# A two-block transformer on one core: the first MLP matrices with both parts of x side by side, and the crossings between layers cut in two

## The chip, the core and the metric

The kernel runs on one NeuronCore of a Trainium2 chip. The metric is the device time of one execution in microseconds (us); lower is better. TensorE multiplies a stationary 128x128 operand (loaded by its own instruction, the weight load) with a moving operand of up to 512 columns and writes to PSUM, whose banks hold 512 fp32 values per partition. VectorE (DVE), ScalarE (ACT) and GpSimd (POOL) do the rest, and SyncE (SP) starts the transfers of the weights.

## The reference, cut to what matters

Two blocks run one after the other on 256 tokens of width 1024. The first has two layers, each a mixer (a convolution with latent attention, then a sparse attention) followed by an MLP; the second puts 16 meta tokens in front and has two more layers. Everything is float32. What the change touches is the MLP and the step between two layers:

```python
def sq_relu_mlp(x, w1, w2):
    h = jax.nn.relu(x @ w1)
    return (h * h) @ w2
...
        x = x + rms_norm(m, norm_mix_post[layer])
        h = rms_norm(x, norm_mlp_pre[layer])
        x = x + rms_norm(sq_relu_mlp(h, mlp_w1[layer], mlp_w2[layer]), norm_mlp_post[layer])
```

w1 is 1024x4096 and w2 is 4096x1024; there are two such MLPs.

## The kernel before

**Products in parts.** For accuracy each fp32 number a is split into a high part (rounded to the format fp32r that TensorE takes) and a low part (the rest), and a product is the sum of three: high by high, high by low, low by high. `mm3` issues these three. Each weight tile of 128x1024 comes in by DMA, ScalarE rounds it to its high part (L288) and VectorE subtracts to get the low one (L289). `Stream` keeps four such tiles ready.

**The MLP** (`mlp`, from L606). Activations stand transposed: 128 features on the partitions, 256 tokens in the columns, in eight slices `xh[:, k]` and `xl[:, k]`. The hidden layer has 16 pieces j of 256 features. For one piece, two tiles m times eight slices k times three products of 256 columns run into one PSUM bank "d" (`take2`, 48 products). `hidden` then squares what is positive (Relu and Square on ScalarE, a product and a subtraction on VectorE) and leaves the high and low operands `hh`, `hl`. `acc_block` multiplies a piece with its rows of w2: 24 products of 512 columns into four accumulators in the "w" banks. Pieces 0 to 3 are made before the first `acc_block`; from then on piece j+1 is made ahead of `acc_block` j. In the last block the four accumulators finish one after the other (two halves of the tokens, two halves of the features), and `done` has ScalarE square each with a sum (L479).

**The crossing** (`cross`). When a layer's product is complete, each half of the tokens (t = 0, 1: 128 tokens each) is normalised, transposed back on TensorE and added to x, and from the new x come the next layer's `xh`, `xl`. For a half: VectorE adds the sums into `q` (L501 or L503), GpSimd raises it to -1/2 (L504), ScalarE and VectorE scale one 256-column half each of the two accumulators (L506, L508, and DVE calls by the helper at L493), TensorE does eight 128-column transposes into two banks (L514), `busy` puts idle products of 512 columns behind the last real one (2 in the first half, 4 in the second), and VectorE adds eight 128-column pieces to x (helper `after`, L493: it keeps VectorE's calls in the written order). All eight adds of the first half stand ahead of the second half's scaling. Then, slice by slice, ScalarE makes `xh` (L527) and VectorE `xl`.

There are four crossings: 1 from the first layer into the first MLP, 2 from that MLP into the third layer, 3 from the third layer into the second MLP, 4 from that MLP into the second block.

**The order of the work.** Each engine runs its own queue in order. The queues are laid out when the program is built, by a scheduler that goes by the written order and by estimated times, so an instruction that it expects to be ready late is put behind later ones.

**Where xh and xl live.** Two tiles with one buffer each, allocated by `xg("xh", ...)` and `xg("xl", ...)`.

## Time and profile before

| | us |
|---|---|
| median of three runs | 980.37 |
| lowest and highest | 979.43, 981.09 |
| the profiled execution, its own time | 979.38 |
| its span, from the first to the last instruction | 977.6 |

The span lies 1.8 us inside the execution's own time. Busy time of an engine is a union of its instructions' times; TensorE's instructions overlap each other, so the time from one start to the next, not an instruction's length, is what a product costs.

### The profile page before, as it was taken

How to read it: one execution, taken by the hardware profiler on the slowest of the kernel's cores; microseconds unless marked ns; L12 is line 12 of the kernel's file. 1: busy time of each engine (PE TensorE's matmuls, PEld its weight loads, DVE VectorE, ACT ScalarE, POOL GpSimd, SP SyncE). 2: the span in 40 equal slices, each digit the busy share in tenths (PEclk: the TensorE clock that was granted, in tenths of full speed). 3: DMA queues.
4: the chain of work that ended last, by engine and by line, in shares of the span. 5: the costliest groups of instructions: out<-in, count | busy, mean ns of one | idle time of the engine just before them, and what ended most of it. 6: DMA issues, size and time to landing. Idle time of an engine off the chain costs nothing.

```text
span 977.6 us, 17239 instructions
## 1 busy us (share of the span) xinstructions
PE 950.6 (97%) x6674; PEld 852.8 (87%) x6674; DVE 662.5 (68%) x1358; ACT 513.6 (53%) x929; POOL 83.6 (9%) x117
## 2 busy tenths in 40 slices
PE   7999999999999999998999999999999999999996
PEld 6999879999998898876989999978898789998985
DVE  6889567555554999983855555567988757657762
ACT  6646456444444677773744444454535435363442
POOL 1121000000000100000000000000211210005121
PEclk9999999999999999999999999999999999999999
DMA  9754436655554455430666555536354314633201
GB/s 333 250 172 151 134 126 234 223 187 186 193 190 138 144 193 154 141 103 1 203 210 194 188 187 187 191 103 248 110 183 141 120 45 145 221 130 129 89 2 43
DMA packets 46066, 154.52 MB, mean 158 GB/s; under 512 B 6424, under 2 KB 7968, under 8 KB 45856
## 3 DMA queue, kind: packets, MB, share of 16 engines
q1 hardware_dynamic: 45552, 152.85, 47.6%
q8 instruction: 52, 0.85, 0.3%
q10 hardware_dynamic: 432, 0.57, 0.2%
q14 instruction: 30, 0.25, 0.1%
HBM read 152.34 MB, written 2.70 MB: 159 GB/s over the span
## 4 chain that ended last, share of the span: by engine, by line
PE 94%; ACT 2%; DVE 2%; issue 1%; DMA 1%; POOL 0%; SPq 0%; POOLq 0%; ACTq 0%
PE pd L327 47%; PE pw L327 38%; PE pm L327 5%; PE pm L1133 1%; DVE x L493 1%; PE pm L1165 1%; ACT st L288 1%; DMA x<-in_xT 1%; PE pm L1521 0%; PE pw L514 0%; PE pm L1723 0%; PE pm L514 0%; PE pw L875 0%; ACT sq L479 0%; ACT pm L1119 0%
## 5 line engine op out<-in xcount | busy, mean ns | idle before, releaser
L289 DVE TENSOR_TENSOR st<-st,st 128x1024 fp32r<-128x1024 f32 (+2 forms) x274 | 330.0, 1214 | 161.2 <-ACT st L288 160.6
L288 ACT ACTIVATE st<-st 128x1024 fp32r<-128x1024 f32 (+2 forms) x274 | 282.1, 1042 | 271.7 <-PE pd L327 164.2
L327 PE MATMUL pd<-xh,st 128*128 128x256 f32 (+1 forms) x1856 | 360.2, 289 | 9.1 <-ACT st L288 6.1
L327 PEld LDWEIGHTS pd<-xh,st 128*128 128x128 f32 x1856 | 297.3, 192 | 16.8 <-ACT st L288 6.1
L327 PE MATMUL pd<-xl,st 128*128 128x256 f32 (+1 forms) x928 | 267.5, 289 | 0.0
L327 PEld LDWEIGHTS pd<-xl,st 128*128 128x128 f32 x928 | 178.2, 192 | 3.8 <-issue 0.9
L327 PE MATMUL pw<-st,hh 128*128 128x512 f32 x512 | 157.4, 390 | 0.0
L327 PEld LDWEIGHTS pw<-st,hh 128*128 128x128 f32 x512 | 94.3, 188 | 18.1
L327 PE MATMUL pw<-st,hl 128*128 128x512 f32 x256 | 98.9, 389 | 0.0
L327 PE MATMUL pd<-akq,st 128*128 128x272 f32 (+1 forms) x384 | 78.0, 293 | 0.0
L327 PE MATMUL pw<-xh,st 128*128 128x256 f32 (+1 forms) x384 | 73.6, 286 | 0.0
L327 PEld LDWEIGHTS pd<-akq,st 128*128 128x128 f32 x384 | 61.0, 189 | 2.3 <-issue 1.9
L327 PEld LDWEIGHTS pw<-xh,st 128*128 128x128 f32 x384 | 61.0, 190 | 0.5 <-issue 0.3
L327 PEld LDWEIGHTS pw<-st,hl 128*128 128x128 f32 x256 | 48.1, 188 | 10.3
L327 PE MATMUL pd<-gs,st 128*128 128x272 f32 (+1 forms) x192 | 55.3, 288 | 0.0
L327 PE MATMUL pw<-xl,st 128*128 128x256 f32 (+1 forms) x192 | 54.8, 286 | 0.0
L388 POOL TENSOR_TENSOR rc<-rc,mhalf 128x2 f32<-128x2 f32 (+4 forms) x13 | 13.9, 1074 | 307.0 <-DVE rc L385 307.0
L327 PE MATMUL pw<-st,mh 128*128 128x512 f32 x128 | 38.0, 402 | 1.3 <-ACT mh L339 1.3
L327 PEld LDWEIGHTS pw<-xl,st 128*128 128x128 f32 x192 | 36.5, 190 | 0.2 <-DVE xl L493 0.2
L327 PEld LDWEIGHTS pd<-gs,st 128*128 128x128 f32 x192 | 36.2, 189 | 0.5 <-issue 0.4
L1119 ACT ACTIVATE pm<-pm,st 128x128 f32<-128x128 f32 (+1 forms) x64 | 28.4, 446 | 4.4 <-DVE st L1117 4.3
L327 PEld LDWEIGHTS pw<-st,mh 128*128 128x128 f32 x128 | 23.3, 188 | 6.9 <-ACT mh L339 2.2
(465 smaller groups left out, 1282.7 us busy)
## 6 DMA issues: line engine op xcount, KB each, us to landing
st<-in_w SPq DMA_DIRECT2D x128, 512.0 KB, 4.6
st<-in_ab_in SPq DMA_DIRECT2D x32, 512.0 KB, 4.3
st<-in_cd_in SPq DMA_DIRECT2D x28, 512.0 KB, 4.3
st<-in_a_in SPq DMA_DIRECT2D x18, 512.0 KB, 6.5
st<-in_c_in SPq DMA_DIRECT2D x16, 512.0 KB, 4.7
st<-in_a_out SPq DMA_DIRECT2D x8, 512.0 KB, 4.9
st<-in_c_out SPq DMA_DIRECT2D x8, 512.0 KB, 4.5
st<-in_ab_out SPq DMA_DIRECT2D x8, 512.0 KB, 4.3
```

What stands on the lines that cost most here:

```text
L288: self.last = self.nc.scalar.activation(hi[:, p], raw[:, p], AF.Copy).ins
L289: self.nc.vector.tensor_tensor(lo[:, p], raw[:, p], hi[:, p].bitcast(F32), op=OP.subtract)
L327: self.pe = self.nc.tensor.matmul(out, lhsT, rhs, start=start, stop=stop, skip_group_check=True).ins
L388: nc.gpsimd.tensor_tensor(r, r, self.mhalf[:p, :n], op=OP.pow)
L493: prev = f(*args, **kw).ins
L1119: nc.scalar.activation(o, o, AF.Exp, scale=-1.0, bias=st[:, 0, t, b:b + 1], accum_out=st[:, 1, t, b:b + 1])
L1133: nc.tensor.transpose(tp[:, 128 * j:128 * j + 128], src, self.ident)
L1165: nc.tensor.transpose(ps[:b - a, 128 * j:128 * j + 128], x[:, a:b], self.ident)
```

## The change

In both MLPs, pieces 4 to 15 of the hidden layer are made by a new function `wide`. `xh` and `xl` become the two halves of one tile `xx`, so that one product of 512 columns gives high-by-high in the first half of a bank and high-by-low in the second; low-by-high stays a product of 256 columns. Each of the two tiles m has a bank of its own, and its two halves are added on the way out. Relu and square become one VectorE instruction.

In the crossings, the first half's scaling and transposes (`turn(0)`) are issued by `done` as soon as the first two accumulators are squared, in the written order ahead of the last accumulators' products. Both scalings of the first half are whole 512-column instructions on VectorE; in the second half ScalarE does one and VectorE the other. There are three idle products in place of six. Three of the first half's adds stand ahead of the second half, the other five are spread over the slices.

```diff
-BUSY = (2, 4)
+BUSY, EARLY = 3, 3
...
-    def xg(self, tag, dt, n):
-        t = self.xgp.tile([128, 8 * T2], dt, tag=tag, name=tag)
-        return t[:, :8 * n].rearrange("p (k n) -> p k n", k=8)
+    def xg(self, dt, n):
+
+        t = self.xgp.tile([128, 2, 8 * T2], dt, tag="xx", name="xx")
+        self.xx = t[:, :, :8 * n].rearrange("p a (k n) -> p a k n", k=8)
+        return self.xx[:, 0], self.xx[:, 1]
...
         self.ms.append((m, acc))
...
+        if i == 1:
+            self.scratch = self.psum("d")
+            self.half = self.turn(0)
+
+    def turn(self, t):
+
+        nc = self.nc
+        q = self.np_.tile([128, 8], F32, tag="rc", name="rc", bufs=6)[:, :1]
+        a, b = self.sums[:, 2 * t:2 * t + 1], self.sums[:, 2 * t + 1:2 * t + 2]
+        if self.post[2]:
+            nc.vector.scalar_tensor_tensor(q, a, b, self.eps[:, t:t + 1], op0=OP.add, op1=OP.add)
+        else:
+            nc.vector.tensor_scalar(q, a, b, EPS, op0=OP.add, op1=OP.add)
+        nc.gpsimd.tensor_tensor(q, q, self.mhalf[:, :1], op=OP.pow)
+        (m0, a0), (m1, a1) = self.ms[2 * t:2 * t + 2]
+
+        if t:
+            nc.scalar.activation(m0, a0, AF.Copy, scale=q)
+        else:
+            nc.vector.tensor_scalar(m0, a0, q, None, op0=OP.mult)
+        self.scaled = nc.vector.tensor_scalar(m1, a1, q, None, op0=OP.mult).ins
+        ps = [self.psum("mw"[t]) for _ in range(2)]
+        for p, m in zip(ps, (m0, m1)):
+            for k in range(4):
+                nc.tensor.transpose(p[:, 128 * k:128 * k + 128], m[:, 128 * k:128 * k + 128], self.ident)
+        return ps
...
+        self.busy(BUSY)
+        first = self.half
+        for k in range(EARLY):
+            new(0, first, k)
+        second = self.turn(1)
+        prev = self.scaled
         self.sqs, self.tiles = [], (T_SEQ, meta)
-        new(0)
-        new(1)
+        both = lambda k: [new(0, first, k) for _ in range(k >= EARLY)] + [new(1, second, k)]
+        both(0)
+        both(1)
         for k in range(8):
             if k < 6:
-                new(k + 2)
+                both(k + 2)
...
+            def wide(j):
+
+                hi, lo = self.st.take()
+                a = mp.tile([128, 2, SEQ], F32, tag="a", name="a")
+                for m in range(2):
+                    z = self.psum("d").rearrange("p (t n) -> p t n", t=2)
+                    for k in range(8):
+                        s = slice((m * 8 + k) * 128, (m * 8 + k) * 128 + 128)
+                        self.mm(z, hi[:, s], xx[:, :, k], k == 0, False)
+                        self.mm(z[:, 0], lo[:, s], xh[:, k], False, k == 7)
+                    c = mp.tile([128, SEQ], F32, tag="zc", name="zc")
+                    nc.scalar.activation(c, z[:, 1], AF.Copy)
+                    nc.vector.tensor_tensor(a[:, m], z[:, 0], c, op=OP.add)
+                h = mp.tile([128, 2, SEQ], F32, tag="h", name="h")
+                nc.vector.scalar_tensor_tensor(h, a, 0.0, a, op0=OP.max, op1=OP.mult)
+                hh = mp.tile([128, 2, SEQ], F32R, tag="hh", name="hh", bufs=4)
+                hl = mp.tile([128, 2, SEQ], F32R, tag="hl", name="hl", bufs=4)
+                self.hilo(hh, hl, h)
+                hs[j] = (hh, hl)
...
                 if 4 <= j + 1 < 16:
-                    hidden(j + 1, self.take2(1, xh, xl)[0])
+                    wide(j + 1)
...
-            mh, ml = self.xg("xh", F32R, T2), self.xg("xl", F32R, T2)
+            mh, ml = self.xg(F32R, T2)
...
-            xh, xl = self.xg("xh", F32R, SEQ), self.xg("xl", F32R, SEQ)
-            x = self.cross(x, gain((2, 4, 6)[j]), xh, xl, eps=self.eps if j % 2 else None)
+            xh, xl = self.xg(F32R, SEQ)
+            x = self.cross(x, gain((2, 4, 6)[j]), xh, xl)
```

The other uses of `xg`, in the second block's layers, take the two halves of the one tile in the same way.

## Rows read from the trace of the kernel before

**Rows 1.** The profile page, part 1 (busy us, share of the span, instructions of each engine) and the engines' shares of part 4 (the chain of work that ended last).

```profile
PE 950.6 (97%) x6674; PEld 852.8 (87%) x6674; DVE 662.5 (68%) x1358; ACT 513.6 (53%) x929; POOL 83.6 (9%) x117
...
PE 94%; ACT 2%; DVE 2%; issue 1%; DMA 1%; POOL 0%; SPq 0%; POOLq 0%; ACTq 0%
```

**Rows 2.** The chain of work that ended last, in order of time: start us, length us, what ran, and how many instructions. A block of the first MLP's first matrix and one of its second matrix; the two last blocks of the second matrix; a piece in the second block's first layer whose products have 272 columns.

```profile
176.71 5.70 PE pd L327 x48
182.41 5.46 PE pw L327 x24
...
305.17 10.91 PE pw L327 x48
...
714.39 6.21 PE pd L327 x48
```

**Rows 3.** The timeline of crossing 1 (from the first layer into the first MLP): start us, length us, engine, line, operation, output<-input, shapes, count, and in brackets the idle time before it with what ended it.

```profile
127.56 0.55 POOL L504 TENSOR_TENSOR rc<-rc,mhalf 128x1 f32<-128x1 f32 x1 [14.51 <-DVE rc L501]
...
129.07 1.52 PE L327 MATMUL pd<-st 128*128 128x512 f32 x6
129.27 0.60 ACT L479 ACTIVATE sq<-pw 128x512 f32<-128x512 f32 x1
...
129.99 0.21 DVE L501 TENSOR_SCALAR rc<-ss 128x1 f32<-128x1 f32 x1
...
130.28 0.55 POOL L504 TENSOR_TENSOR rc<-rc,mhalf 128x1 f32<-128x1 f32 x1 [2.17 <-DVE rc L501]
130.43 1.03 PE L514 MATMUL pm<-cg,sq 128*128 128x128 f32 x8
130.87 0.48 ACT L506 ACTIVATE sq<-pw,rc 128x256 f32<-128x256 f32 x1 [0.91 <-POOL rc L504]
...
131.29 1.39 DVE L493 SCALAR_TENSOR_TENSOR x<-pm,gains,x 128x128 f32<-128x128 f32 x5 [1.08 <-PE pm L514]
...
133.36 0.87 DVE L493 TENSOR_SCALAR sq<-pw,rc 128x256 f32<-128x256 f32 x2
...
134.37 0.87 DVE L493 SCALAR_TENSOR_TENSOR x<-pw,gains,x 128x128 f32<-128x128 f32 x3
...
135.31 0.65 PE L327 MATMUL pd<-xh,st 128*128 128x256 f32 x2 [0.59 <-ACT xh L527]
```

**Rows 4.** Busy time by stretch, around the first products behind crossings 1, 2, 3 and 4: for each engine busy us and instructions, then the granted TensorE clock (1.00 is 2.4 GHz, 0.50 is 1.2 GHz), the DMA engines' share and GB/s.

```profile
134.00:140.00 6.00, 5.41 (x29) 4.81 (x30) 5.80 (x17) 5.16 (x12) 0.00 (x0) 0.72 0.23 93
320.00:326.00 6.00, 5.39 (x38) 4.39 (x39) 5.80 (x18) 4.69 (x11) 0.00 (x0) 1.00 0.00 0
462.00:468.00 6.00, 5.39 (x31) 5.10 (x31) 5.94 (x18) 5.80 (x13) 0.00 (x0) 0.72 0.00 0
650.00:656.00 6.00, 6.00 (x35) 5.68 (x35) 6.00 (x17) 5.61 (x13) 0.00 (x0) 0.72 0.46 147
```

**Rows 5.** The timeline of TensorE alone, behind crossing 1, while the clock is at 1.2 GHz.

```profile
136.86 0.41 PE L327 MATMUL pd<-xh,st 128*128 128x256 f32 x1
137.07 0.41 PE L327 MATMUL pd<-xl,st 128*128 128x256 f32 x1
```

**Rows 6.** Groups of instructions by line and shape, from 148.6 to 315.9 us (the first MLP): busy us, mean ns of one, idle before.

```profile
L618 DVE TENSOR_TENSOR h<-a 128x512 f32<-128x512 f32 x16 | 10.9, 684 | 0.0
L621 ACT ACTIVATE hh<-a 128x512 fp32r<-128x512 f32 x16 | 10.1, 632 | 0.4
...
L616 ACT ACTIVATE a<-pd 128x512 f32<-128x512 f32 x14 | 8.1, 580 | 0.0
```

**Rows 7.** Busy time by stretch, 50 us of the first MLP; columns as in rows 4.

```profile
200.00:250.00 50.00, 50.00 (x332) 46.05 (x332) 27.23 (x26) 23.33 (x27) 0.00 (x0) 1.00 0.58 190
```

**Rows 8.** The timelines of ScalarE and of VectorE at the last block of the first MLP: the start and the end of what makes its last pair of operands.

```profile
306.05 0.58 ACT L616 ACTIVATE a<-pd 128x512 f32<-128x512 f32 x1
...
308.11 0.69 DVE L622 TENSOR_TENSOR hl<-h,hh 128x512 fp32r<-128x512 f32 x1
```

**Rows 9.** The timeline of crossing 2 (from the first MLP into the third layer).

```profile
315.91 1.52 PE L327 MATMUL pd<-st 128*128 128x512 f32 x6
...
316.27 1.95 POOL L915 MEMSET kl<- 64x1024 f32 x2 [0.42 <-PE pw L327]
...
318.88 0.54 POOL L504 TENSOR_TENSOR rc<-rc,mhalf 128x1 f32<-128x1 f32 x1
...
322.16 0.51 PE L327 MATMUL pd<-xh,st 128*128 128x256 f32 x2 [0.59 <-ACT xh L527]
```

**Rows 10.** The timeline of crossing 3 (from the third layer into the second MLP).

```profile
455.25 1.53 PE L327 MATMUL pd<-st 128*128 128x512 f32 x6
...
456.34 0.54 POOL L504 TENSOR_TENSOR rc<-rc,mhalf 128x1 f32<-128x1 f32 x1 [5.57 <-DVE rc L501]
...
457.20 0.21 DVE L501 TENSOR_SCALAR rc<-ss 128x1 f32<-128x1 f32 x1 [0.94 <-ACT sq L479]
...
462.67 0.50 PE L327 MATMUL pd<-xh,st 128*128 128x256 f32 x2 [0.59 <-ACT xh L527]
```

**Rows 11.** The timeline of crossing 4 (from the second MLP into the second block).

```profile
644.01 1.53 PE L327 MATMUL pd<-st 128*128 128x512 f32 x6
...
645.29 0.54 POOL L504 TENSOR_TENSOR rc<-rc,mhalf 128x1 f32<-128x1 f32 x1 [2.25 <-DVE rc L503]
...
650.26 0.39 PE L327 MATMUL pw<-xh,st 128*128 128x272 f32 x1
```

More of the change, by code (lines that the diff above doesn't have):

```diff
@@ L486, in cross @@
+    def cross(self, x, g2, xh, xl, meta=None):
+        nc = self.nc
+        g, name = self.post[:2]
         if name:
             self.xn = self.xt(SEQ, name)
-        xn, prev = self.xn, None
+        xn, prev = self.xn, self.scaled
         def after(f, *args, **kw):
             nonlocal prev
-            with self.tc.issue_after(prev) if prev is not None else nullcontext():
+            with self.tc.issue_after(prev):
                 prev = f(*args, **kw).ins
-        self.scratch = self.psum("d")
@@ L496, in cross @@
-        for t, banks in enumerate(("mm", "ww")):
-            q = self.np_.tile([128, 8], F32, tag="rc", name="rc", bufs=6)[:, :1]
-            a, b = self.sums[:, 2 * t:2 * t + 1], self.sums[:, 2 * t + 1:2 * t + 2]
-            if eps is None:
-                nc.vector.tensor_scalar(q, a, b, EPS, op0=OP.add, op1=OP.add)
-            else:
-                nc.vector.scalar_tensor_tensor(q, a, b, eps[:, t:t + 1], op0=OP.add, op1=OP.add)
-            nc.gpsimd.tensor_tensor(q, q, self.mhalf[:, :1], op=OP.pow)
-            (m0, a0), (m1, a1) = self.ms[2 * t:2 * t + 2]
-            nc.scalar.activation(m0[:, 0:256], a0[:, 0:256], AF.Copy, scale=q)
-            after(nc.vector.tensor_scalar, m0[:, 256:512], a0[:, 256:512], q, None, op0=OP.mult)
-            nc.scalar.activation(m1[:, 0:256], a1[:, 0:256], AF.Copy, scale=q)
-            after(nc.vector.tensor_scalar, m1[:, 256:512], a1[:, 256:512], q, None, op0=OP.mult)
-            ts = slice(128 * t, 128 * t + 128)
-            ps = [self.psum(c) for c in banks]
-            for h, (p, m) in enumerate(zip(ps, (m0, m1))):
-                for k in range(4):
-                    nc.tensor.transpose(p[:, 128 * k:128 * k + 128], m[:, 128 * k:128 * k + 128], self.ident)
-            self.busy(BUSY[t])
-            new = lambda k: after(nc.vector.scalar_tensor_tensor, xn[:, k, ts], ps[k // 4][:, 128 * (k % 4):128 * (k % 4) + 128],
-                                  g[:, k:k + 1], x[:, k, ts], op0=OP.mult, op1=OP.add)
-            if t == 0:
-                for k in range(8):
-                    new(k)
@@ L521, in cross, with new @@
+        def new(t, ps, k):
+            ts = slice(128 * t, 128 * t + 128)
+            after(nc.vector.scalar_tensor_tensor, xn[:, k, ts], ps[k // 4][:, 128 * (k % 4):128 * (k % 4) + 128],
+                  g[:, k:k + 1], x[:, k, ts], op0=OP.mult, op1=OP.add)
+        self.busy(BUSY)
[4 more added lines that the diff above has]
+        prev = self.scaled
         self.sqs, self.tiles = [], (T_SEQ, meta)
-        new(0)
@@ L1566, in layer_cd @@
             nc.sync.dma_start(ccd, self.i["ccd"])
-            big = self.xg("xl", F32, T2).rearrange("p a b -> p (a b)")
+            place, big = [v.rearrange("p a b -> p (a b)") for v in self.xg(F32, T2)]
             dect, ck = [big[:, a:b].rearrange("p (k n) -> p k n", n=T2) for a, b in ((0, 4 * T2), (4 * T2, 6 * T2))]
@@ L1583, in layer_cd @@
             nc.gpsimd.memset(zero, 0.0)
-            big = self.xg("xh", F32, T2).rearrange("p a b -> p (a b)")
-            dkr = big[:, :4 * T2].rearrange("p (k n) -> p k n", n=T2)
-            dq = big[:, 4 * T2:4 * T2 + 4 * SEQ].rearrange("p (k n) -> p k n", n=SEQ)
+            dkr = place[:, :4 * T2].rearrange("p (k n) -> p k n", n=T2)
+            dq = place[:, 4 * T2:4 * T2 + 4 * SEQ].rearrange("p (k n) -> p k n", n=SEQ)
             ps = [self.psum(b)[:, :T2] for b in "ddwwww"]
@@ L1865, in run @@
         for j in range(4):
-            self.post = (gain(4 * (j // 2) + 1 + 2 * (j % 2)), f"x{j + 1}" if j < 3 else None)
+            self.post = (gain(4 * (j // 2) + 1 + 2 * (j % 2)), f"x{j + 1}" if j < 3 else None, j % 2 == 1)
             if j == 0:
```

9 lines of the change are left out of this document (4 added, 5 removed).

## The prediction

> **What bounds the kernel now.** First read the page: TensorE is busy for 97% of the span, and 94% of the chain that ended last is TensorE's [rows 1]. So the time is what the products cost, plus the places where TensorE stands or runs slowly. Two views show which are which. The chain in order of time shows the MLP as an unbroken alternation: 48 products of 256 columns in 5.70 us, 24 of 512 columns in 5.46 us [rows 2]. In 50 us of it TensorE is busy for all 50, while VectorE has 27.2 us of work and ScalarE 23.3 [rows 7]: here only cheaper products help. Then the timeline of crossing 1, read on VectorE's rows [rows 3]: the last product gives way to the idle ones at 129.07 us, the next layer's first product starts at 135.31, and between them lie 1.4 us of idle products, 16 transposes and waiting. The chain through this hole is VectorE's: eight adds of the first half from 131.29, then the second half's scaling at 133.36, whose factor had been there since 130.28 + 0.55 = 130.83. Last, the clock [rows 4]: behind crossings 1, 3 and 4 the mean granted clock of six microseconds is 0.72, behind crossing 2 it is 1.00. With two levels, 0.28 x 6 = 1.7 us of full-speed work are lost at each of the three.
>
> **The wide products.** A product starts every 5.70/48 = 118.75 ns at 256 columns and every 5.46/24 = 227.5 ns at 512 [rows 2]. Doubling the columns adds 108.75 ns, so 10 ns of each product do not depend on its columns. For one tile m and slice k, three products (356.25 ns) become one of 512 and one of 256 columns (346.25 ns): 10 ns. There are 2 x 8 of these in a piece, 12 pieces in an MLP, two MLPs: 384 x 10 ns = **3.84 us gained**. The slow clock agrees in kind [rows 5]: at 1.2 GHz a 256-column product starts every 0.21 us, twice 105 ns, so at full speed some 12 ns are not columns.
>
> The Trainium skill (TensorE: Matmul & The Clock Gate, section "Wait — 56ns, not 53.3ns?") gives a warm product N/2.4 ns plus a fixed 2.5 ns or so. By that the term would be 384 x 2.5 ns = 1.0 us. The trace disagrees for these products, each with its own weight load, and I go by the rows.
>
> What before does not show is a moving operand read in two runs of 256 values, as `xx[:, :, k]` is. From above: if the 512-column product lost its fixed 10 ns and more besides, down to twice the 105 ns of the slow clock [rows 5], a pair would take 328.75 ns, a gain of 10.6 us. From below: the nearest row with a dearer 256-column run has 272 columns at 6.21/48 = 129.4 ns [rows 2]; two of these would make 258.8 ns in place of 227.5, a loss of 8.2 us. I take the plain 512-column row, the same size and type.
>
> **The way out of PSUM.** A piece now costs ScalarE 0.58 + 0.63 us and VectorE 0.68 + 0.69 us [rows 6, 8]. Afterwards ScalarE has two 256-column copies (at most 0.48 each, as the scaling at 130.87 [rows 3]) and one rounding, VectorE two 256-column adds (about 0.44 each, half of the 0.87 at 133.36 [rows 3]) and two 512-column instructions: 0.4 and 0.9 us more for a piece of 11.2 us. The 27.2 of 50 us hide that [rows 7], and a "d" bank is used again only one piece later. Cost nothing. The tight place is the last piece, needed 5.46 us after its products end: the block row at 305.17 holds two blocks, so the last begins at 310.63 [rows 2]. Its operands are there at 308.80 [rows 8]; 0.9 to 1.3 us more leaves at least 0.5 us. Without that cover every microsecond would count, twice in the kernel.
>
> The one tile for `xh` and `xl` has to wait for the readers of both parts, but the two parts are read in the same triples of products: at most one product later, nothing. No transfer moves; SyncE's queue keeps its order.
>
> **The crossings.** I follow crossing 1 [rows 3]. The first half's factor is there at 127.56 + 0.55 = 128.11. Two whole scalings on VectorE, at most 0.87 each, are done at 128.98 and 129.85. Three idle products take 3 x 0.2275 = 0.68 from 129.07 to 129.75. The transposes start then; the adds followed them by 0.86 before, so three adds (0.26 apart, 1.39 for five) run from 130.6 to 131.4, while GpSimd works on the second half. The second half's sum is added at 129.99, ahead of these adds: before, too, it was queued ahead of the first half's adds though written behind them, and I keep that order. Its factor is there at 130.83. ScalarE scales 512 columns in 0.60 (as its square at 129.27) from 130.87 to 131.47. Before, the first add of the second half stood 0.57 behind its bank's last scaling (two scalings in 0.87 from 133.36, add at 134.37); with two more transposes, about 0.8. So that add is at 132.27 and the first product 135.31 - 134.37 = 0.94 later, at 133.21: **2.10 gained**. Five adds of 0.26 to 0.34 now fall among the slices; with a slice's `xl` that makes some 1.15 us per slice against 12 products of 118.75 ns = 1.43, so TensorE remains the slower.
>
> From the factor to the first product it is thus 133.21 - 130.83 = 2.38 us. In the other crossings:
>
> - Crossing 2: the factor waits on GpSimd behind the third layer's memsets, which start at 316.27; it starts at 318.88 and takes about 0.54 [rows 9]. That cost nothing while VectorE was later. Now 319.42 + 2.38 = 321.80 against 322.16: 0.36 gained. Should the factor be put ahead of the memsets, it starts 1.21 behind the products' end as in crossing 1, and 2.1 are gained.
> - Crossing 3: all four accumulators end together. The first half's factor is there at 456.34 + 0.54 = 456.88 [rows 10]; both scalings hold VectorE to 458.64, and the second half's sum, at 457.20 before, comes behind them: factor at 459.50, first product at 461.88 against 462.67, 0.79 gained. Between the two scalings it would be 1.66, behind the three adds nothing.
> - Crossing 4: factor at 645.83, product at 648.21 against 650.26 [rows 11]: 2.05 gained.
>
> Together 2.10 + 0.36 + 0.79 + 2.05 = **5.3 us**. If the sum stands behind the adds in 1 and 4 too, the factor comes 1.41 later there: 0.69 + 0.36 + 0 + 0.64 = 1.7. With the better case everywhere 7.9.
>
> **The clock.** What ran before it fell: from the last idle product (0.2275 each behind 129.07, 315.91, 455.25, 644.01) to the first real product, with only transposes and small things in between, passed 4.9 us in crossings 1, 2 and 4 and 6.05 in crossing 3 [rows 3, 9, 10, 11]. It fell in three, and held in one of the three equal ones [rows 4]. Afterwards these stretches are 3.5 in crossings 1 and 4, 5.2 in crossing 2, 5.95 in crossing 3. I take it that 1 and 4 keep the clock, 3 loses it as before, and 2, now longer than two that fell, loses it: 2 x 1.68 - 1.68 = **1.7 us gained**, between a loss of 1.7 (only 2 changes) and a gain of 5.0 (none falls).
>
> **The sum.** 3.84 + 5.3 + 1.7 = 10.8 us off the profiled execution's 979.38, so 968.5. The median of the runs lies 0.99 above that execution; for a median I add 1.0: **969.5**.
>
> **The rivals.**
>
> - The sum of the second half queued behind the three adds: crossings 1.7 in place of 5.3, time 973.1. Against it speaks the order before in all four crossings; for it, that the adds are now ready earlier. Chance 0.17.
> - Transposes queued too early: the diff writes them ahead of the last accumulators' products, and if the scheduler puts all eight before the last three products (start 128.16), TensorE stands until 128.98, and after the second bank's at 129.85 + 0.4 has lost some 2.1 us; everything behind moves with it. Crossings 1 and 4 then gain nothing, crossing 2 loses 1.7, crossing 3 keeps 0.79; with 3.84 and the clock held in 1 and 4 time is about 975. Against it: before, these transposes sat behind all six idle products though their data were there (scaling at 128.5 to 129.85). Chance 0.13.
> - The 10 ns are not saved: a 512-column product over two runs costs what two products of 256 cost, 237.5 ns, and the wide products give nothing: 969.5 + 3.84 = 973.3. For it, no product of before reads two runs; against it, the 512-column products [rows 2]. The skill's 2.5 ns, named above, would give 972.3. Chance 0.08.
> - No crossing loses the clock and the queues come out well: 3.84 + 7.9 + 5.0, time 963.6. Chance 0.13.
> - Slower: the two-run operand stalls the 512-column product. It decides from 237.5 + 7000/384 = 256 ns a product on, where it eats the crossings' 7 us too; at the rate of 1.2 GHz, 420 ns, the time would be 1043. No row shows such an operand, and each run is 1 KB in one piece. Chance 0.05. The Trainium skill (Advanced Engine Details and Errata, section "Memory Cachelines") warns that a non-contiguous pattern slows products; it says so of PSUM, where the output here is one whole bank, and no row of before shows it for the moving operand.
>
> The forecast itself has 0.44, within 966 to 973. About 0.2% (2 us) is what a measurement here tells from no change. Faster by more: the forecast, the first, third and fourth rival, most of the second, 0.90; within 0.2%: 0.04 from the second rival's worse orders and a mild stall; slower: 0.06. Leaving out half of the best case and what lies beyond the second rival, the range is 963.5 to 976.5.
>
> **What would show it.** In the MLP, a block of the first matrix should take 16 x 346 ns = 5.54 us in the chain in place of 5.70, with TensorE never idle. In crossing 1 the first product should start some 4.1 us behind the last product, not 6.2; in crossing 2 the GpSimd power should end last. The clock should read 1.00 behind crossings 1 and 4. I am wrong if the 512-column product starts later than every 230 ns, if TensorE waits for the transposes ahead of its last products, or if the factor's sum stands behind the adds on VectorE.

## The result and the profile after

The changed kernel takes **970.39 us** (median of four runs, 969.29 to 973.12) against 979.90 for the kernel before, measured beside it: a ratio of 0.9905, 95% interval 0.9891 to 0.9919. The forecast was 969.5. Six later runs of the same kernel, beside later runs of the kernel before (981.01), gave 974.43 (969.65 to 976.29; ratio 0.9916, 0.9885 to 0.9947). Both intervals lie clear of 1, so the gain of almost 1% is real; how much of it one execution shows depends on the clock and on one wait, both below. Medians of different experiments were not all taken side by side, so a ratio, or a stage of a profile, compares better than a median.

The profiled execution has 970.29 us, its span 968.5 against 977.6, so 9.1 us went. The page, parts 1 and 4 as in [rows 1]:

```profile
PE 941.0 (97%) x6278; PEld 829.2 (86%) x6278; DVE 679.2 (70%) x1402; ACT 510.6 (53%) x941; POOL 83.7 (9%) x117
...
PE 91%; DVE 2%; DMA 2%; ACT 2%; issue 1%; POOL 1%; SPq 0%; POOLq 0%; ACTq 0%; DVEq 0%
```

TensorE is still 97% busy, but the chain now has 2% of DMA in place of 1%: some work waits for weights that did not before. Where the time went is read by cutting the span at the first idle product and the first real product of each crossing (both are rows of the timeline). The same cuts were made in every experiment, so the table serves all of this document. Times in us, of one profiled execution each; e1 to e11 and e13 are the experiments below (e7, without idle products, has no such cut and is left out).

| kernel | start | crossing 1 | MLP 1 | crossing 2 | third layer | crossing 3 | MLP 2 | crossing 4 | second block | span |
|---|---|---|---|---|---|---|---|---|---|---|
| before | 129.07 | 6.24 | 180.60 | 6.25 | 133.09 | 7.42 | 181.34 | 6.25 | 327.33 | 977.6 |
| **after** | 128.78 | 4.18 | 178.72 | 5.91 | 135.68 | 6.50 | 178.65 | 4.45 | 325.63 | 968.5 |
| e1 wide products alone | 130.13 | 6.25 | 178.45 | 6.24 | 135.44 | 7.43 | 179.16 | 7.09 | 326.23 | 976.4 |
| e2 crossings alone | 128.38 | 4.18 | 179.10 | 5.92 | 134.97 | 6.24 | 179.77 | 4.39 | 329.46 | 972.4 |
| e3 two products | 130.07 | 4.18 | 179.10 | 6.28 | 134.22 | 6.70 | 181.45 | 4.45 | 327.60 | 974.0 |
| e4 one run | 127.94 | 4.18 | 177.18 | 6.37 | 135.48 | 6.24 | 177.83 | 4.45 | 329.98 | 969.7 |
| e5 power first | 128.83 | 4.18 | 177.18 | 4.55 | 135.46 | 6.23 | 177.98 | 4.39 | 327.77 | 966.6 |
| e6 fill | 130.35 | 4.19 | 177.26 | 5.91 | 135.56 | 6.24 | 177.99 | 4.46 | 328.67 | 970.6 |
| e8 bias queue | 130.25 | 4.18 | 177.18 | 5.91 | 135.56 | 6.70 | 178.17 | 4.45 | 324.18 | 966.6 |
| e9 one tile | 129.21 | 6.24 | 181.74 | 6.25 | 135.29 | 7.43 | 180.91 | 6.25 | 326.81 | 980.1 |
| e10 crossings, two tiles | 129.65 | 4.19 | 179.17 | 5.92 | 134.85 | 6.23 | 179.91 | 4.39 | 331.55 | 975.9 |
| e11 both repairs | 128.08 | 4.18 | 177.19 | 4.55 | 134.93 | 6.23 | 177.84 | 4.39 | 323.73 | 961.1 |
| e13 after again | 129.23 | 4.18 | 177.27 | 5.91 | 135.57 | 6.69 | 179.86 | 4.44 | 329.89 | 973.0 |

Read the crossing columns first: they hardly move from kernel to kernel with the same crossing, since they are set by a fixed chain of instructions. The exceptions are crossings in which the clock fell before they ended: 7.09 in e1, 6.28 and 6.37 in crossing 2 of e3 and e4, 6.50 to 6.70 in crossing 3. The long stages move by 1 to 4 us between kernels with the same products, and that is the clock and the waits.

**A block of the MLP**, in the chain in order of time (start, length), answers to [rows 2]:

```profile
174.40 5.56 PE pd L327 x32
179.96 5.44 PE pw L327 x24
```

Thirty-two products (16 of 512 and 16 of 256 columns) take 5.56 us where 48 took 5.70. No wait of TensorE stands in this MLP. The last operand of its last block, answers to [rows 8]:

```profile
304.95 0.69 DVE L340 TENSOR_TENSOR hl<-h,hh 128x512 fp32r<-128x512 f32 x1 [0.70 <-ACT hh L339]
```

**Crossing 1**, its timeline, answers to [rows 3]:

```profile
127.85 0.75 DVE L502 TENSOR_SCALAR sq<-pw,rc 128x512 f32<-128x512 f32 x1 [0.66 <-POOL rc L496]
...
128.78 0.84 PE L327 MATMUL pd<-st 128*128 128x512 f32 x3
...
129.46 1.03 PE L507 MATMUL pm<-cg,sq 128*128 128x128 f32 x8
...
129.70 0.21 DVE L495 TENSOR_SCALAR rc<-ss 128x1 f32<-128x1 f32 x1 [0.44 <-ACT sq L481]
...
129.99 0.55 POOL L496 TENSOR_TENSOR rc<-rc,mhalf 128x1 f32<-128x1 f32 x1 [2.17 <-DVE rc L495]
130.09 0.87 DVE L521 SCALAR_TENSOR_TENSOR x<-pm,gains,x 128x128 f32<-128x128 f32 x3 [0.18 <-PE pm L507]
...
132.96 1.26 PE L327 MATMUL pd<-xx,st 128*128 128x256 f32 x5 [0.55 <-ACT xx L541]
```

The first transposes stand behind the three idle products, not among the last real ones; the second half's sum (129.70) stands ahead of the three adds (130.09), which run while GpSimd takes the power. From that power's end (130.54) to the first product are 2.42 us.

**Crossing 2**, GpSimd's part of the timeline, answers to [rows 9]:

```profile
312.04 1.95 POOL L951 MEMSET kl<- 64x1024 f32 x2 [0.42 <-PE pw L327]
...
314.64 0.54 POOL L496 TENSOR_TENSOR rc<-rc,mhalf 128x1 f32<-128x1 f32 x1
...
317.59 0.51 PE L327 MATMUL pd<-xx,st 128*128 128x256 f32 x2 [0.55 <-ACT xx L541]
```

The power is last, behind memsets of the third layer, as forecast.

**Crossing 3**, answers to [rows 10]: the first half's two scalings, the second half's power and its transposes.

```profile
454.93 0.75 DVE L502 TENSOR_SCALAR sq<-pw,rc 128x512 f32<-128x512 f32 x1 [0.65 <-POOL rc L496]
...
455.60 0.74 DVE L503 TENSOR_SCALAR sq<-pw,rc 128x512 f32<-128x512 f32 x1
...
456.54 0.54 POOL L496 TENSOR_TENSOR rc<-rc,mhalf 128x1 f32<-128x1 f32 x1 [1.64 <-DVE rc L495]
...
457.86 1.78 PE L507 MATMUL pw<-cg,sq 128*128 128x128 f32 x8 [0.74 <-ACT sq L500]
```

The eight transposes take 1.78 us because the clock has fallen by then: from 457.8 to 459.8 us it reads 0.58. In e2, where it held, they take 1.09:

```profile
457.15 1.09 PE L507 MATMUL pw<-cg,sq 128*128 128x128 f32 x8 [0.74 <-ACT sq L500]
```

**Crossing 4**, answers to [rows 11]: the second half's power, two products of 400 columns that the second block puts ahead of its first real one, and that first product.

```profile
639.76 0.54 POOL L496 TENSOR_TENSOR rc<-rc,mhalf 128x1 f32<-128x1 f32 x1 [2.31 <-DVE rc L493]
...
642.10 0.83 PE L327 MATMUL pw<-cab,ab_s 32*8 32x400 f32 x2
...
642.87 0.39 PE L327 MATMUL pw<-xx,st 128*128 128x272 f32 x1
```

**The clock**, in stretches behind the four crossings (PEclk is the number ahead of the DMA share), answers to [rows 4]:

```profile
132.00:138.00 6.00, 5.43 (x31) 4.99 (x30) 5.93 (x19) 4.57 (x10) 0.00 (x0) 0.72 0.54 218
318.00:324.00 6.00, 5.98 (x38) 5.89 (x38) 6.00 (x19) 4.74 (x11) 0.00 (x0) 0.72 0.01 3
459.00:465.00 6.00, 5.87 (x40) 5.44 (x40) 5.94 (x20) 4.58 (x10) 0.00 (x0) 0.79 0.01 3
643.00:649.00 6.00, 6.00 (x50) 6.00 (x51) 6.00 (x19) 4.39 (x11) 0.00 (x0) 1.00 0.38 115
```

It fell behind 1, 2 and 3 and held behind 4: not the forecast's pattern (hold behind 1 and 4). Three falls were there before, three are there now.

**The second block**, TensorE's longest wait in its first 50 us, and the transfer that the chain shows ahead of it:

```profile
PE pm L327 <- DVE nz L1266: 2.3, 1, 2.3
```

```profile
656.50 7.47 DMA st<-in_ab_in
664.08 1.07 ACT st L288
```

Before, this wait had 0.2 us. ScalarE's row of norms, which `nz` needs, stands in its queue behind a weight rounding (L288), and the rounding's weights arrive at 663.97.

### The profile page after: what moved, and what is told of

Read it like the earlier page. It is cut to its first block, busy times and chain, and to the rows that moved or that the text cites. A ratio compares the mean times of both kernels' runs of the same rounds, so it can differ in the third digit from the quotient of the medians.

```text
span 968.5 us, 16486 instructions
## 1 busy us (share of the span) xinstructions
PE 941.0 (97%) x6278; PEld 829.2 (86%) x6278; DVE 679.2 (70%) x1402; ACT 510.6 (53%) x941; POOL 83.7 (9%) x117
## 4 chain that ended last, share of the span: by engine, by line
PE 91%; DVE 2%; DMA 2%; ACT 2%; issue 1%; POOL 1%; SPq 0%; POOLq 0%; ACTq 0%; DVEq 0%
PE pd L327 46%; PE pw L327 37%; PE pm L327 5%; PE pm L1169 1%; DMA st<-in_ab_in 1%; DMA x<-in_xT 1%; PE pm L1201 1%; DVE st L289 1%; ACT st L288 1%; DMA st<-in_w 0%; PE pw L507 0%; PE pm L1557 0%; DVE pm L1153 0%; ACT pm L1155 0%; ACT sq L500 0%
## 5 line engine op out<-in xcount | busy, mean ns | idle before, releaser
L288 ACT ACTIVATE st<-st 128x1024 fp32r<-128x1024 f32 (+2 forms) x274 | 282.3, 1043 | 270.0 <-PE pd L327 150.7
L327 PE MATMUL pd<-xx,st 128*128 128x256 f32 (+2 forms) x2400 | 362.8, 307 | 8.9 <-ACT st L288 6.3
L327 PEld LDWEIGHTS pd<-xx,st 128*128 128x128 f32 x2400 | 329.2, 192 | 34.6 <-ACT st L288 6.3
L327 PE MATMUL pw<-xx,st 128*128 128x256 f32 (+1 forms) x576 | 74.8, 284 | 0.0
L327 PEld LDWEIGHTS pw<-xx,st 128*128 128x128 f32 x576 | 70.9, 189 | 1.0 <-ACT xx L541 0.7
L496 POOL TENSOR_TENSOR rc<-rc,mhalf 128x1 f32<-128x1 f32 x8 | 4.3, 542 | 210.0 <-DVE rc L493 186.1
L327 PE MATMUL pw<-st,ml 128*128 128x512 f32 x64 | 22.2, 403 | 0.0
L481 ACT ACTIVATE sq<-pw 128x512 f32<-128x512 f32 x16 | 9.5, 598 | 23.0 <-PE pw L327 23.0
L653 DVE TENSOR_TENSOR a<-pd,zc 128x256 f32<-128x256 f32 x48 | 20.1, 418 | 0.0
```

The costliest lines, as they stand in the source:

```text
L288: self.last = self.nc.scalar.activation(hi[:, p], raw[:, p], AF.Copy).ins
L327: self.pe = self.nc.tensor.matmul(out, lhsT, rhs, start=start, stop=stop, skip_group_check=True).ins
L481: self.last = self.nc.scalar.activation(m, acc, AF.Square, scale=1.0 / 32, accum_out=self.sums[:, i:i + 1]).ins
L496: nc.gpsimd.tensor_tensor(q, q, self.mhalf[:, :1], op=OP.pow)
L653: nc.vector.tensor_tensor(a[:, m], z[:, 0], c, op=OP.add)
```

## The experiments

### Are the wide products worth 10 ns each? (e1, e3, e4)

**e1** has the new `wide` with the crossings of before.

```diff
-BUSY, EARLY = 3, 3
+BUSY = (2, 4)
...
-        if i == 1:
-            self.scratch = self.psum("d")
-            self.half = self.turn(0)
...
-            x = self.cross(x, gain((2, 4, 6)[j]), xh, xl)
+            x = self.cross(x, gain((2, 4, 6)[j]), xh, xl, eps=self.eps if j % 2 else None)
```

> The wide products alone, with the crossings as before. Theory (each product carries about 10 ns that do not depend on its columns): a block of the first matrix takes 5.56 us in the chain in place of 5.70, a pair of blocks 11.00 in place of 11.16, the four crossings stay at 6.2, 6.2, 7.4 and 6.2 us from the last product to the next layer's first, and the time is 979.4 - 3.84 = 975.5 us, a ratio of 0.996. Rival (nearly all of the gain is the crossings'): blocks between 5.56 and 5.70 but time at 978.5 or more.

**e3** is the changed kernel with each wide product issued as two.

```diff
-                        self.mm(z, hi[:, s], xx[:, :, k], k == 0, False)
+                        self.mm(z[:, 0], hi[:, s], xh[:, k], k == 0, False)
+                        self.mm(z[:, 1], hi[:, s], xl[:, k], False, False)
```

> The changed kernel with the 512-column product written as two of 256 columns into the same two halves of the same bank; banks, the way out of PSUM and everything else stay. Theory (a cost per product): a block goes from 5.56 back to about 5.70 us and the time rises by 24 x 0.16 = 3.8 us to 974.1. Rival (the saving comes from one bank per tile or from the other way out, not from fewer products): the block stays at 5.56 us and the time at 970.3.

**e4** lays `xx` out so that the 512 values of a slice are one run.

```diff
-        self.xx = t[:, :, :8 * n].rearrange("p a (k n) -> p a k n", k=8)
+        if n == SEQ:
+            self.xx = t.rearrange("p a b -> p (a b)")[:, :16 * n].rearrange("p (k a n) -> p a k n", k=8, a=2)
+        else:
+            self.xx = t[:, :, :8 * n].rearrange("p a (k n) -> p a k n", k=8)
```

> The changed kernel with both parts of a slice next to each other, so that the moving operand of 512 columns is one run and not two of 256. Theory (two runs cost nothing): a block stays at 5.56 us, time 970.3 within 1 us. Rival (the second run costs something): the block falls below 5.54 us; if the whole surplus over twice the slow-clock rate were the run's, to 5.3 us, and the time by 5 us or more.

Measured: e1 977.09 us (ratio 0.9949, 0.9925 to 0.9973), e3 975.37 (0.9929, 0.9904 to 0.9955), e4 973.02 (0.9895, 0.9856 to 0.9934). A block of each in the chain, e1, then e3, then e4:

```profile
177.55 5.56 PE pd L327 x32
```

```profile
174.16 5.70 PE pd L327 x48
```

```profile
172.02 5.56 PE pd L327 x32
```

Splitting the product again brings the 5.70 back, whatever the crossing; the operand in two runs costs nothing, since one run takes the same 5.56. A block and its partner fall from 5.70 + 5.46 to 5.56 + 5.44, 0.16 us, and 24 pieces give 24 x 0.16 = 3.84. The table says the same of a whole MLP: of the profiles in which the clock held in MLP 1, the six with wide products have 177.18 to 177.27 us (e4, e5, e6, e8, e11, e13), the three without 179.10 to 179.17 (e2, e3, e10): 1.9 us for each MLP.

The times themselves are less sharp. e1 lies 3.9 us below the kernel before beside it (980.95), as the theory had it, but its median missed the 975.5 by 1.6, and its crossing 4 took 7.09 in place of 6.2, since the clock fell inside it. e3 missed its 974.1 by 1.3, and its interval overlaps that of the change. e4 missed 970.3 by 2.7, with a ratio like that of the change.

### What do the crossings and their idle products do? (e2, e7, e5, e6)

**e2** has the new crossings and the old MLP products.

```diff
-                    wide(j + 1)
+                    hidden(j + 1, self.take2(1, xh, xl)[0])
```

> The new crossings alone, with every piece of the hidden layer made by three products of 256 columns. Theory: blocks of the first matrix back at 5.70 us, the crossings at 4.2, 5.9, 6.5 and 4.45 us as in the changed kernel, time 970.3 + 3.84 = 974.1 us, a ratio of 0.9946. Rival (the two parts help each other, for instance through where the clock falls): more than 2 us away from 974.1.

Measured: 975.86 (0.9920, 0.9891 to 0.9950). Its crossings are as short as in after, 4.18, 5.92, 6.24 and 4.39 us, so they owe nothing to the products. The time lies within the 2 us of the theory. By medians e1 gains 3.9 us and e2 5.1 over the kernel before beside them, together 9.0; the change gains 9.5, in its later runs 6.6. As far as this scatter lets one see, the two parts add up.

**e7** leaves the three idle products out.

```diff
-        self.busy(BUSY)
```

> The changed kernel without any idle products. Theory: the crossings are as long as before or up to 0.4 us shorter each, since the first half's transposes no longer stand behind three idle products; but the stretch without products grows by 0.7 us, so the clock should fall behind crossing 4 too, which costs 1.7 us: time 970.5 to 972. Rival (the idle products do nothing for the clock): clock 1.00 behind crossing 4 as in the changed kernel, time 969 to 970.3.

Measured: 972.55 (0.9900, 0.9863 to 0.9937), 0.5 us above the expected range. The clock fell behind crossings 2, 3 and 4 and held behind 1; behind crossing 4, where every kernel with the new crossing and its idle products held it, the stretch reads:

```profile
643.00:649.00 6.00, 6.00 (x34) 5.16 (x33) 5.94 (x18) 4.69 (x10) 0.00 (x0) 0.72 0.16 47
```

But leaving the idle products out did more than that. From one product (0.23 us) behind the start of the last real one to the next layer's first, crossings 1 and 4 take 4.68 and 4.88 us, not shorter, as expected, but 0.5 and 0.4 longer. In crossing 1 the three adds start 0.64 us behind the last real product (at 129.45) in place of 1.31 in after, and the second half's sum now stands behind them:

```profile
130.09 0.87 DVE L521 SCALAR_TENSOR_TENSOR x<-pm,gains,x 128x128 f32<-128x128 f32 x3
...
130.87 0.20 DVE L495 TENSOR_SCALAR rc<-ss 128x1 f32<-128x1 f32 x1
```

So the hole behind crossing 4 grew as well, the clock held behind crossing 1 without any idle product, and there is one profile of this kernel. That the idle products keep the clock behind crossing 4 fits it and is not shown by it.

**e5** puts GpSimd's power ahead of the third layer's memsets (three more, `zz`, `hd` and `kbd`, are treated alike).

```diff
-        nc.gpsimd.tensor_tensor(q, q, self.mhalf[:, :1], op=OP.pow)
+        self.pow = nc.gpsimd.tensor_tensor(q, q, self.mhalf[:, :1], op=OP.pow).ins
...
-                nc.gpsimd.memset(kl.bitcast(F32)[HALVES[1 - gg], :, gg], 0.0)
+                with tc.issue_after(self.pow):
+                    nc.gpsimd.memset(kl.bitcast(F32)[HALVES[1 - gg], :, gg], 0.0)
```

> The changed kernel with the third layer's memsets on GpSimd put behind the second half's power in crossing 2. Theory (in crossing 2 the power behind the memsets sets the end): the crossing goes from 5.9 to about 4.2 us, 1.7 us gained there. The clock behind it then either holds (another 1.7 gained, time about 967) or falls as before (time about 968.6). Rival (VectorE or the transposes set the end): crossing 2 stays within 0.3 us of 5.9, time 970.3.

Measured: 971.38 (0.9891, 0.9852 to 0.9930). GpSimd's rows in crossing 2:

```profile
311.79 0.54 POOL L496 TENSOR_TENSOR rc<-rc,mhalf 128x1 f32<-128x1 f32 x1 [1.65 <-DVE rc L493]
...
312.39 1.95 POOL L952 MEMSET kl<- 64x1024 f32 x2
```

The crossing takes 4.55 us in place of 5.91, 1.36 less, and the clock holds behind it. It is 0.35 short of the expected 4.2: the power starts 1.60 us behind the first idle product (310.19), not 1.21, since the sum ahead of it stands behind the first half's second scaling on VectorE (from 310.84). The time missed the expected 967. With the crossing shorter and the clock held the third layer still takes 135.46 us, and the second block gives 2.1 us back at a longer wait for `nz` (2.9 us), where the clock fell.

**e6** fills the holes with idle products behind the transposes too (and nine in place of three in crossing 3).

```diff
-BUSY, EARLY = 3, 3
+BUSY, MID, END, EARLY = (3, 3, 9, 3), (4, 4, 4, 4), (2, 2, 2, 0), 3
...
-        self.busy(BUSY)
+        at = self.post[3]
+        self.busy(BUSY[at])
+        with self.tc.issue_after(self.tr):
+            self.busy(MID[at])
...
+        with self.tc.issue_after(self.tr):
+            self.busy(END[at])
```

> The changed kernel with idle products of 512 columns also behind the first half's transposes (4) and behind the second half's (2, not in crossing 4), and 9 in place of 3 ahead of the first transposes in crossing 3. Theory (the clock falls for want of products in the crossing): the granted clock reads 1.00 behind crossings 1 and 3 at least, perhaps 2, and the time falls by up to 1.7 us for each that held, to 966 to 968, less some tenths where an idle product delays a transpose. Rival (the clock falls for another reason): 0.72 over six microseconds as before, time 970 to 971.

Measured: 972.98 (0.9902, 0.9866 to 0.9938). No fall behind any crossing, with crossings as long as before the filling. Yet it is no faster than after, and misses the expected 966 to 968: the second block lost the clock instead, at the wait for `nz` (its row, and the stretch behind it):

```profile
PE pm L327 <- DVE nz L1271: 2.4, 1, 2.4
```

```profile
668.00:674.00 6.00, 6.00 (x28) 5.61 (x28) 1.88 (x3) 0.71 (x1) 0.00 (x0) 0.58 0.55 210
```

### Why is part of it handed back in the second block? (e8)

SyncE's queue holds, ahead of the weights, a read (`tm`) of a bias table that is first written to DRAM (`d<-d`). The queue in after:

```profile
645.61 0.56 SPq L1231 DMA_DIRECT2D d<-d  x1
653.75 0.33 SPq L1503 DMA_DIRECT2D tm<-d  x1
654.14 0.41 SPq L1539 DMA_DIRECT2D tt<-d  x1
654.65 0.38 SPq L280 DMA_DIRECT2D st<-in_ab_in  x1
```

From 646.17 to 653.75, 7.6 us, nothing is issued. **e8** moves the reads to GpSimd's queue.

```diff
-        nc.sync.dma_start(tm, skew[0:16, :, 144:160])
+        nc.gpsimd.dma_start(tm, skew[0:16, :, 144:160])
...
-            nc.sync.dma_start(tt, skew[:, h])
+            nc.gpsimd.dma_start(tt, skew[:, h])
```

> The changed kernel with the reads of the bias table in the second block's first layer issued from GpSimd's queue and not from SyncE's. Theory (the weights of that layer stand in SyncE's queue behind the first of these reads, which waits for the table to be written out, and so TensorE waits 2.3 us for the row of norms that ScalarE makes behind the late weights): the first weight transfer behind crossing 4 starts 2 to 4 us earlier, the 2.3 us wait disappears, time about 968. Rival (the wait has another cause, or comes back behind other work): time within 1 us of 970.3.

Measured: 968.41 (0.9867, 0.9831 to 0.9904). Its queue and its wait:

```profile
645.14 0.56 SPq L1231 DMA_DIRECT2D d<-d  x1
651.50 9.50 SPq L280 DMA_DIRECT2D st<-in_ab_in  x8
```

```profile
PE pm L327 <- DVE nz L1266: 0.7, 1, 0.7
```

Counted from the first product behind crossing 4, the weights go out 9.1 us on in place of 11.8 (651.50 - 642.40, 654.65 - 642.87); the wait shrinks from 2.3 to 0.7 us and the second block from 325.63 to 324.18. So the wait is one for weights, and the time came out as expected. The read is not all that holds them: in e8 the queue still stands from 645.70 to 651.50. Before, they went out just as late, 11.9 us on (662.13 - 650.26), but TensorE, at half its clock there, came later too:

```profile
661.71 0.33 SPq L1467 DMA_DIRECT2D tm<-d  x1
662.13 0.37 SPq L280 DMA_DIRECT2D st<-in_ab_in  x1
```

### Why is the third layer longer? (e9, e10)

In every kernel above the third layer takes 134.2 to 135.7 us, 133.09 before. **e9** is the kernel before with the one tile for `xh` and `xl` alone; **e10** is e2 with two tiles.

```diff
-    def xg(self, tag, dt, n):
-        t = self.xgp.tile([128, 8 * T2], dt, tag=tag, name=tag)
-        return t[:, :8 * n].rearrange("p (k n) -> p k n", k=8)
+    def xg(self, dt, n):
+
+        t = self.xgp.tile([128, 2, 8 * T2], dt, tag="xx", name="xx")
+        self.xx = t[:, :, :8 * n].rearrange("p a (k n) -> p a k n", k=8)
+        return self.xx[:, 0], self.xx[:, 1]
```

> The kernel before with nothing but xh and xl as the two halves of one tile: products of 256 columns throughout, crossings as before. In every kernel run so far that has the one tile, the third layer takes 134.2 to 135.7 us against 133.09 before, whatever its crossing. Theory (the one tile gives a part of the gain back: what reads or writes one part is ordered against the other, and the third layer's queues come out worse): third layer 134.5 to 135.5 us, execution 981 to 983. Rival (the third layer is longer because its crossing ends earlier than its weights and vector work can follow, the tile costs nothing as predicted): third layer 133.1 us and 980 as before.

```diff
-        t = self.xgp.tile([128, 2, 8 * T2], dt, tag="xx", name="xx")
-        self.xx = t[:, :, :8 * n].rearrange("p a (k n) -> p a k n", k=8)
-        return self.xx[:, 0], self.xx[:, 1]
+        t = [self.xgp.tile([128, 8 * T2], dt, tag=f"x{c}", name=f"x{c}")[:, :8 * n].rearrange("p (k n) -> p k n", k=8) for c in "hl"]
+        self.xx = None
+        return t[0], t[1]
```

> The crossings of the change alone (all MLP products 256 columns wide), with xh and xl in two tiles as before. With one tile this was 975.9, its third layer 134.97 us. Theory (the tile is to blame): third layer about 133.1 to 133.5 us, plus 1.7 if the clock falls in it, and some 974 in all. Rival (the earlier crossing is to blame): third layer 135 us and 975.9 as with one tile.

Measured: e9 981.04 (1.0017, 0.9988 to 1.0045), e10 975.21 (0.9938, 0.9917 to 0.9959). The third layers, 135.29 and 134.85, look like a verdict against the tile in e9 and against the crossing in e10. They are neither. e2 and e10 differ in the tile alone, and have 134.97 and 134.85. The row of norms, the first product in this layer that needs more than `xh`, `xl` and weights, in before, e9, e10, after and e11:

```profile
336.29 0.61 PE L327 MATMUL pm<-cg,rc 128*128 128x128 f32 x4
```

```profile
339.77 0.60 PE L327 MATMUL pm<-cg,rc 128*128 128x128 f32 x4
```

```profile
335.13 0.60 PE L327 MATMUL pm<-cg,rc 128*128 128x128 f32 x4
```

```profile
336.87 0.61 PE L327 MATMUL pm<-cg,rc 128*128 128x128 f32 x4
```

```profile
331.73 0.61 PE L327 MATMUL pm<-cg,rc 128*128 128x128 f32 x4
```

Behind the layer's first product that is 14.13 us in before, 16.33 in e9, 16.20 in e10, 19.28 in after and 17.73 in e11. In e9 and e10 the clock fell right there, for e9 all through these six microseconds:

```profile
323.00:329.00 6.00, 5.66 (x26) 5.54 (x26) 5.94 (x17) 5.91 (x13) 0.00 (x0) 0.50 0.00 0
```

e9's row is 2.2 us behind that of before, and the whole layer is 2.2 us longer: nothing is added behind the row, its excess is the clock's. e1, with the old crossing as well, has the same fall (0.50 from 321 to 327 us) and 135.44. e11 kept the clock and is late all the same. The laid-out queues tell why: between the crossing and this row there are 112 products of 256 columns in before, e1 and e9, 117 in e2, e3 and e10, but 144 in after, e5 and e11. Thirty-two products of 118.75 ns are 3.8 us, about the 3.6 that e11's row is late. So the tile is innocent and so is the crossing alone: wide products and crossings together make the scheduler put the row of norms, and all that hangs on it, 32 products later. In e2 and e10 the excess without the fall's 1.7 us is next to nothing (134.97 - 1.7 = 133.27, 134.85 - 1.7 = 133.15); with the late row it is 1.8 to 2.5 with the clock held (e5, e6, e11). And with the late row the fall adds nearly nothing: after, e8 and e13, where the clock fell at the start of this layer, take 135.56 to 135.68, e5 and e6, where it held, 135.46 and 135.56. These five and e11 also have a wait of TensorE for VectorE (`qt`, 0.8 to 0.9 us, some 47 us into the layer) that before and e2 do not have. That the late row is what costs these 2 us is argued from this; no kernel moved the row alone.

### The two repairs together, and the change once more (e11, e13)

**e11** has the edits of e5 and e8.

> The change with both repairs that paid by themselves: GpSimd's power ahead of its memsets in crossing 2, and the reads of the bias table on GpSimd's queue instead of SyncE's. If the two are independent: crossing 2 is 4.55 us instead of 5.91, the second block about 324.2 instead of 325.6, and about 1.4 + 1.5 us less than the change, 967 to 968. If the shorter crossing is given back in the third layer: as with the bias reads alone, 968.4.

Measured: **965.41** (962.90 to 967.76; ratio 0.9833, 0.9805 to 0.9860), better than both kernels and 1.6 us better than expected. Crossing 2 has the expected 4.55 and the second block 323.73. In the profiled execution the clock is 1.00 behind all four crossings, and TensorE's wait for `nz` is back at what before had:

```profile
PE pm L327 <- DVE nz L1269: 0.2, 1, 0.2
```

**e13** is the changed kernel, unaltered.

> The changed kernel once more, not altered, for a second profiled execution. Theory (where the clock falls behind crossing 1 is a matter of the single execution, since six kernels with the same crossing kept it): 970.4, and the clock keeps 1.00 behind crossing 1, with about 1.7 us less in the first MLP (177.2 us instead of 178.7). Rival (this kernel's own schedule makes it fall there): the fall is again behind crossing 1, MLP 178.7 us.

Measured: 974.43. Behind crossing 1, and at the wait in the second block:

```profile
132.00:138.00 6.00, 5.44 (x44) 4.99 (x43) 5.55 (x18) 4.58 (x10) 0.00 (x0) 1.00 0.60 241
...
666.00:672.00 6.00, 2.73 (x9) 2.05 (x10) 5.98 (x12) 2.31 (x3) 0.81 (x2) 0.68 1.01 412
```

```profile
PE pm L327 <- DVE nz L1266: 4.1, 1, 4.1
```

The clock held behind crossing 1, as the theory had it, and MLP 1 took 177.27. But TensorE stood 4.1 us for `nz`, the clock fell there, and the second block took 329.89 against 325.63: the expected 970.4 failed on that. Why the wait was longer stands in SyncE's queue:

```profile
655.67 0.33 SPq L1503 DMA_DIRECT2D tm<-d  x1
```

The write of the bias table goes out 2.75 us behind the block's first product in all kernels with the new crossing, but the read that waits for it went out 12.5 us behind that product here (655.67 - 643.15) and 10.9 in after (653.75 - 642.87). The profiles with this read on SyncE and the clock held behind crossing 4 fall into the same two groups: 10.8 to 11.0 us in after, e3, e5 and e6, with waits for `nz` of 2.3 to 2.9 us, and 12.3 to 12.5 in e2, e4, e10 and e13, with 3.9 to 4.8. In e8 and e11, whose weights do not stand behind the read, they go out 9.1 us on in both. Why the write takes longer in some executions no run shows.

The six runs follow the mean granted clock: 969.65 and 971.45 at 0.993, 974.03 to 976.29 at 0.991 and 0.989.

## Why the prediction was right, and where it was not

**The wide products: right.** 3.84 us forecast; 24 x 0.16 = 3.84 measured, with e3 taking the block's share of it away again. The Trainium skill (TensorE: Matmul & The Clock Gate, section "Wait — 56ns, not 53.3ns?") has a fixed part of 2.5 ns; here the runs show 10, and the rows were the better guide. The warning of the Trainium skill about non-contiguous patterns in PSUM (Advanced Engine Details and Errata, section "Memory Cachelines") does not reach this moving operand: two runs and one run both take 5.56 us.

**The way out of PSUM and the one tile: right.** TensorE never waits in MLP 1, and e9 is no slower than before. The last block of MLP 1 begins at 311.68 - 5.44 = 306.24; its last operand is there at 304.95 + 0.69 = 305.64, 0.6 us earlier, where at least 0.5 was forecast.

**The crossings: right in the chain of each, two of them mis-sized.** Forecast 2.10, 0.36, 0.79 and 2.05; measured 2.06, 0.34, 0.92 and 1.80, together 5.1 of 5.3. In crossing 4 the stretch from power to product, forecast as the 2.38 of crossing 1, is 642.87 - 640.30 = 2.57: the two products of 400 columns stand in between. In crossing 3 the agreement is in part luck: the first half's two scalings took 1.41 us (454.93 to 456.34) where the forecast gave them twice 0.87, and with the clock held the crossing gains 1.18 (7.42 less 6.24 in e2); in the profiled execution the fall inside the hole took 0.26 of that back. The rival on early transposes fell with the timeline above. The rival on the order of sum and adds fell there too, but e7 shows that order, and there, without the idle products ahead of the adds, it cost 0.4 to 0.5 us a crossing where the prediction gave it 1.41. e5 shows 1.70 us (6.25 less 4.55) where the prediction gave 2.1 to a power ahead of the memsets.

**The clock: wrong in the profiled execution, right for crossings 1 and 4 in most others.** Forecast was 1 and 4 held, 2 and 3 lost, net 1.7; with three falls before and three after, the profiled execution had a net of nothing. In the ten profiled executions with the new crossing and its idle products (after, its repeat, e2 to e6, e8, e10 and e11), crossing 4 held in all and crossing 1 in all but one, the profiled execution of after. MLP 1 shows the price: 178.72 there, 177.27 in the repeat. It was lost behind crossing 2 in all of them except e5, e6 and e11, which shorten or fill it; crossing 3 went either way. So the term for crossing 1 (1.7) held in nine of ten executions and was missing from the one that was profiled first. The charge for crossing 2 (1.7 lost, because before held the clock there) rests on one execution of before: in e1 and e9, which have the crossings of before, the clock fell behind crossing 2 as well, and behind the other three.

**What the prediction lacked.** It took the stages behind the crossings as unchanged, and two are not. The third layer was to lose 1.7 to the clock and lost 2.6; with the clock held it still loses 1.8 to 2.5, as far as is argued above for the row of norms placed later. In the second block the clock held behind crossing 4, but the 1.7 us went into the wait for `nz`: from the first product to the product that uses `nz` it takes 24.12 us before (674.38 in its chain) and 24.45 after. The prediction named SyncE's queue as unmoved, which was so but for one read of the table (`tt`) that now goes out ahead of the first weights, and did not ask what a TensorE that arrives earlier would meet there. Against this, the rest of the second block came out 2.0 us shorter (303.2 before, 301.2 after, 301.4 in e11); no run isolates why.

**The sum.** By stage, forecast and measured gain in the profiled execution: crossings 5.3 and 5.12; MLP 1 3.60 and 1.88; MLP 2 1.92 and 2.69, its fall lying partly in the hole; third layer -1.68 and -2.59; second block 1.68 and 1.70; start 0 and 0.29. That is 10.8 and 9.1. The median lies within 1 us of the forecast; two of its agreements (the third layer and the second block) are close for reasons other than those it gave. The forecast of the profiled execution, 968.5, was 1.8 us too low; that of the median was only 0.9 off because the 1.0 us added for a median, which before showed, did not appear (970.29 and 970.39). That is luck, and the repeat at 974.43 shows how far the same kernel can lie from it.

## What to carry to other kernels

Count a product by the time from one start to the next at two sizes: the difference gives the part that merging saves, here 10 ns for each merged pair. When a hole on the busiest engine is shortened, look at the next row that the engine must wait for, and at what is queued ahead of its weights; a gain that arrives there early is given back in the wait. Before a gain or a loss is put down to the clock, profile more than one execution: here the first profile of each kernel showed a pattern that others of the same crossings did not repeat. Two small edits to queues (a power ahead of memsets, weights not behind a dependent read) brought the ratio from 0.9905 and 0.9916 to 0.9833, nearly as much again as the change itself.

## What the runs showed of the hardware

- The same kernel loses the clock in different places from one execution to the next. Crossing 1, with the same instructions, read 0.72 over six microseconds in one execution of after and 1.00 in another; the six runs of the repeat spread over 6.6 us and follow their mean granted clock. A fall inside a crossing stretches it: eight transposes took 1.78 us in place of 1.09.
- A long wait in a busy stage can cost more than itself. Where TensorE stood 2.3 us for `nz` in after, the clock held and the second block took 325.63; where it stood 4.1 us in the repeat, or 2.4 in e6, the clock fell (means of 0.68 and 0.58 over six microseconds there) and the block took 329.89 and 328.67. In e2, e3, e4, e5 and e10, with waits of 2.4 to 4.8 us, it fell at that place too.
- One stalled read holds back the transfers queued behind it on SyncE: 7.6 us without an issue in after, and in e8, without the read ahead of them, the weights go out 2.7 us earlier, counted from the crossing. How long it stalls differs by 1.6 us from one execution of the same kernel to the next (10.9 and 12.5 us behind the first product).
